# Forgetting attention: the values of two groups of heads in one GEMM, and two paddings

## The chip, the cores and the metric

The kernel runs on one core of one Trainium2 chip. The metric is the device time of one execution in microseconds. A core has TensorE (PE in the profile, its weight loads PEld), VectorE (DVE), ScalarE (ACT), GpSimd (POOL) and SyncE (SP), each with its own queue, and DMA engines.

## What is computed

One layer on 512 tokens of width 1024, all in float32: a modulated FFN, a mixing layer with two branches (an mLSTM and a forgetting attention), and a second modulated FFN. The change is in the attention. Cut to it:

```python
z = u @ w_mix + b_mix                      # q_f, k_f, v_f: 16 heads of 64 each
def forgetting_attention(q, k, v, f_pre, q_g, k_g):
    q = rms_norm(q, q_g); k = rms_norm(k, k_g)
    F = cumsum(log_sigmoid(f_pre))         # over the tokens
    logits = q @ k.T / 8 + (F[query] - F[key])      # causal
    p = softmax(logits)
    return p @ v
```

The FFN is `(silu(u @ w_a) * (u @ w_b)) @ w_out`.

## The kernel before

**Numbers.** A float32 product is made of three fp32r products: each operand is split into a high and a low part (`split`, L96 on ACT and L98 on DVE for weights), and `mm3` (L115 to L117) issues high x high, high x low and low x high into the same PSUM bank. A tile's name with h or l at its end is such a part: `wh`, `wl` are weights, `uh`, `ul` the normalized activations, eight tiles of 128 channels each.

**Buffers.** PSUM is cut in two pools of four banks each, `g` for the large GEMMs and `t` for the small ones. A tile of a pool with a tag shares that tag's buffers with the tiles before it and waits until one is free. Every pool's tiles start where the ones before them end; `pad` takes a few bytes so that later tiles start elsewhere.

**Order.** A scheduler puts each engine's instructions into one fixed order when the kernel is built, from priorities and its own estimate of durations. The program's text gives the priorities: the attention's steps call `advance(fill, n)` between them, which takes `n` steps of a generator of large GEMM pieces, so that PE has work while DVE and ACT do the softmax.

**The first FFN's products.** `pair_out` multiplies ready sums of hidden channels (tiles `ph`, `pl`, and `pt` for the last three pairs) with weights in `product` (L472 to L474). The ready sums are the stationary operand, 128 columns of them, and 512 columns of weights move. The first FFN's tiles lie in pools above the pool `tp` ("f1t"), which holds a `pad` of 96 bytes; the second FFN uses the same code with other pools.

**The attention's groups.** The 16 heads are worked in four groups of four. `fox_qkv(g)` makes a group's tokens-by-channels tiles: first q and k (one GEMM of 512 columns, four chunks of 256 rows of weights), evacuated to `tk` and normalized, then the values (a GEMM of 256 columns in two chunks of 512 rows). `u_gemm_tokens` runs a chunk over four token blocks, with one `g` bank for each block, and yields after every second block; in the last chunk `done` evacuates each bank. For the values that is a bias add on DVE (`vg`, L1110), then for each pair of heads a copy on ACT (`fvt`, L1113) and a subtraction on DVE (L1114), into the tiles `fvt`, which share the tag "vm" (six buffers) with the mLSTM's values `vm`.

**A head.** `fox_t` transposes q and k of two heads (L1144) and splits them (`fq`, `fk`, `klz`; L1146 to L1154), `fox_s` makes scores of a head in four `t` banks (L1173, L1174) and reduces them on DVE (L1176, L1180), `fox_p` scales and transposes the probabilities (L1202) and splits them into `Ph`, `Pl` (L1200, L1201), `fox_o` multiplies with the values (L1232) and adds up (`yt`, `yb`; L1235, L1236).

**The fill.** While the last two mLSTM heads are worked, the fill is `fox_qkv(0)`, in round g of four heads it is `fox_qkv(g + 1)`, and in the last round the gated mLSTM output `y_a`. `with_gates` puts a number of gate GEMMs behind each (`gate`: two steps of twelve matmuls of 512 columns, one `g` bank, a tanh `tg` on ACT, L1268).

Of the kernel before, what the change touches and what calls it, by code (L numbers as in the profile page):

```python
# [11 lines left out]
F32 = mybir.dt.float32  # L12
F32R = mybir.dt.float32r
# [7 lines left out]
P = 128  # L21
T = 512
NT = 4
D = 1024
NK = 8
# [9 lines left out]
QM, KM, VM, OM, IG, FG, QF, KF, VF, FFG, GA, GB = (  # L35
    0, 512, 1024, 2048, 3072, 3076, 3080, 4104, 5128, 6152, 6168, 7192)
# [12 lines left out]
class Layer:  # L49
# [96 lines left out]
    def consts(self, tp):  # L146
        nc, cp, A = self.nc, self.cp, self.A
        row = lambda ap: ap.rearrange("o (r p) -> (o r) p", p=P)
        bm = A["b_mix"]

        self.rowsC = tp.tile([32, P], F32, name="rowsC")
        for r, ap in ((0, row(A["c"])), (8, row(A["ffn1_norm_g"])), (16, row(A["b_ada"][:, 0:2048]))):
            nc.scalar.dma_start(self.rowsC[r:r + ap.shape[0], :], ap)
        self.ident = cp.tile([P, P], F32, name="ident")
        make_identity(nc, self.ident)
        self.one = cp.tile([P, 1], F32, name="one")
        nc.gpsimd.memset(self.one, 1.0)
        self.rowsA = tp.tile([P, P], F32, name="rowsA")
        put = lambda r, ap: nc.gpsimd.dma_start(self.rowsA[r:r + ap.shape[0], :], ap)
        put(R_N2, row(A["mix_norm_g"]))  # L160
        put(R_N3, row(A["ffn2_norm_g"]))
        put(R_CW, A["conv_w"][0].rearrange("j (m p) -> (j m) p", p=P))
        put(R_CB, row(A["conv_b"]))
        put(R_QK, row(bm[:, 0:1024]))
        put(R_GG, row(bm[:, GA:GA + 2048]))
        put(R_MG, A["mlstm_norm_g"][0].rearrange("h (r p) -> (h r) p", p=P))
        put(R_FQ, A["fox_q_norm_g"][0].rearrange("(r h) p -> r (h p)", h=2))
        put(R_FK, A["fox_k_norm_g"][0].rearrange("(r h) p -> r (h p)", h=2))
        put(R_OM, row(bm[:, OM:OM + 1024]))
        self.gbias = cp.tile([96, 1], F32, name="gbias")  # L170
        nc.gpsimd.memset(self.gbias, 0.0)
        for r, o, n in ((0, IG, 4), (32, FG, 4), (64, FFG, 16)):
            nc.gpsimd.dma_start(self.gbias[r:r + n, :], bm[0, o:o + n].unsqueeze(1))

        warm = tp.tile([P, 1], F32, name="warm")
        self.pad(tp, 96)
        nc.scalar.activation(warm, self.one, AF.Silu)
        self.oneR = cp.tile([P, 2, 33], F32R, name="oneR")
        nc.scalar.activation(self.oneR, self.one.unsqueeze(2).to_broadcast([P, 2, 33]), AF.Copy, scale=0.0)
        for h in range(2):  # L180
            nc.scalar.activation(self.oneR[:, h, 32 * h:32 * h + 1], self.one, AF.Copy)
        self.mod_d = self.dp.tile([9, D], F32, name="mod_d")
        self.pad(cp, 64)
# [809 lines left out]
    def v_mlstm(self, half, ap, ip):  # L993
        nc, w = self.nc, self.A["w_mix"][0]
        bb = self.bias_bcast([(VM + half * 512, 512)], ip)
        vt = []
        for i in range(2):
            pair = [self.vp.tile([P, NT, 264], F32R, name=self.nm("vm"), tag="vm", bufs=6)[:, :, 0:258] for _ in range(2)]
            nc.scalar.activation(pair[0][:, :, 256:258], self.onz, AF.Copy)
            nc.scalar.activation(pair[1][:, :, 256:258], self.onz, AF.Copy, scale=0.0)  # L1000
            vt.append(pair)
        def done(tb, ps):
            f = self.tmp(ip, "vf")
            nc.vector.tensor_tensor(f, ps, bb, op=ADD)
            for i in range(2):
                hi, lo = vt[i]
                s = slice(i * 256, (i + 1) * 256)
                nc.scalar.activation(hi[:, tb, 0:256], f[:, s], AF.Copy)
                nc.vector.tensor_tensor(lo[:, tb, 0:256], f[:, s], hi[:, tb, 0:256], op=SUB)
        def mk(ch):  # L1010
            def make():
                wh, wl = self.w_mov(w, ch * 256, VM + half * 512)
                return wh, wl, 2 * ch, 2
            return make
        self.vt[2 * half:2 * half + 2] = vt
        yield from self.u_gemm_tokens([mk(c) for c in range(4)], 512, done)
# [60 lines left out]
    def fox_qkv(self, g, ip):  # L1077

        nc, sp, w = self.nc, self.sp, self.A["w_mix"][0]
        o = g * 256  # L1080
        bb = self.bias_bcast([(QF + o, 256), (KF + o, 256)], ip)
        tok = [ip.tile([P, 512], F32, name=self.nm("tk"), tag="tok", bufs=4) for _ in range(NT)]
        ss = sp.tile([P, NT, 8], F32, name=self.nm("fs"), tag="fs", bufs=2)
        def done(tb, ps):
            nc.vector.tensor_tensor(tok[tb], ps, bb, op=ADD)  # L1085
            j = self.tmp(ip, "fj")
            nc.scalar.activation(j, tok[tb], AF.Square)
            nc.vector.tensor_reduce(ss[:, tb, :], j.rearrange("p (h d) -> p h d", h=8), AX.X, ADD)
        def mk(ch):
            def make():  # L1090
                sh = [P, 2, 512]
                rows = w[ch * 256:(ch + 1) * 256]
                r = self.raw(sh, [(lambda t, i=i: t[:, :, i * 256:(i + 1) * 256],
                                   rows[:, c + o:c + o + 256].rearrange("(k p) n -> p k n", p=P))
                                  for i, c in enumerate((QF, KF))])
                wh, wl = self.split(r, sh)
                return wh, wl, 2 * ch, 2
            return make
        yield from self.u_gemm_tokens([mk(c) for c in range(4)], 512, done)
        v = sp.tile([P, NT * 8], F32, name=self.nm("fv"), tag="fv", bufs=2)  # L1100
        nc.vector.tensor_scalar(v, ss.rearrange("p b h -> p (b h)"), 1.0 / 64, EPS, op0=MUL, op1=ADD)
        r = self.rsqrt(v, NT * 8)
        for tb in range(NT):
            t3 = tok[tb].rearrange("p (h d) -> p h d", h=8)
            nc.vector.tensor_tensor(t3, t3, r[:, tb * 8:(tb + 1) * 8].unsqueeze(2).to_broadcast([P, 8, 64]), op=MUL)
        bv = self.bias_bcast([(VF + o, 256)], ip)
        vt = [self.vp.tile([P, NT, 2, P], F32R, name=self.nm("fvt"), tag="vm", bufs=6) for _ in range(2)]
        def donev(tb, ps):
            f = ip.tile([P, 256], F32, name=self.nm("vg"), tag="t2", bufs=3)
            nc.vector.tensor_tensor(f, ps[:, :256], bv[:, :256], op=ADD)  # L1110
            for pr in range(2):
                f2 = f[:, pr * P:(pr + 1) * P].rearrange("p (h d) -> p h d", h=2)
                nc.scalar.activation(vt[pr][:, tb, :, 0:64], f2, AF.Copy)  # L1113
                nc.vector.tensor_tensor(vt[pr][:, tb, :, 64:P], f2, vt[pr][:, tb, :, 0:64], op=SUB)  # L1114
        def mkv(ch):
            def make():
                sh = [P, 4, 256]
                r = self.raw(sh, [(lambda t: t, w[ch * 512:(ch + 1) * 512, VF + o:VF + o + 256]
                                   .rearrange("(k p) n -> p k n", p=P))])
                wh, wl = self.split(r, sh)  # L1120
                return wh, wl, 4 * ch, 4
            return make
        self.fx[g] = (tok, vt)
        yield from self.u_gemm_tokens([mkv(c) for c in range(2)], 256, donev)

    def fox_t(self, p, ap):

# [168 lines left out]
    def run(self):  # L1296
# [61 lines left out]
        with tc.tile_pool(name="heads", bufs=1) as self.vp, tc.tile_pool(name="att", bufs=1) as ip:  # L1358
# [27 lines left out]
            def with_gates(gen, n):  # L1386
                yield from gen
                for m, i in (next(gates) for _ in range(n)):
                    yield from self.gate(m, i, ip)
            for h0, n, fill in ((0, 3, with_gates(self.v_mlstm(1, ip, ip), 2)), (2, 4, with_gates(self.fox_qkv(0, ip), 2))):  # L1390
                for f, h in ((self.mlstm_w, h0), (self.mlstm_w, h0 + 1), (self.mlstm_h, h0), (self.mlstm_h, h0 + 1)):
                    f(h, ip)
                    advance(fill, n)
                    if f == self.mlstm_h and h == 2:
                        self.fox_t(0, yp)
                advance(fill, 99)
            for n in range(18):
                if n % 4 == 0 and n < 16:
                    advance(fill, 99)
                    g = n // 4  # L1400
                    fill = with_gates(self.fox_qkv(g + 1, ip), 4 if g < 2 else 3) if g < 3 else (s for m in range(NK) for s in self.y_a(m, yp, ip))
                last = n >= 12
                if n < 16:
                    self.fox_s(n, ip)
# [98 lines left out]
```

## Time and profile before

| what | value |
|---|---|
| median of 3 runs | 1333.47 us (1333.05 to 1334.53) |
| profiled execution | 1333.42 us |
| its span | 1331.6 us |
| PE busy | 1312.8 us, 6468 matmuls |
| DVE busy | 945.8 us |
| ACT busy | 631.3 us |

The span is the time from the first to the last instruction of the profiled execution; its own time has some 1.8 us around it. In a group's row stand the line, engine, operation, tiles (result<-operands), shape and count, then busy time in us and the mean duration in ns, then idle time of the engine ahead of it and what ended that. In a timeline row stand start and duration in us, then the same names. In a row of windows stand the window, its length, then busy us (and instructions) of PE, PEld, DVE, ACT and POOL, the clock, the share of the DMA engines and GB/s. Matmuls are pipelined, so that a matmul's record is longer than its distance to the next.

### The profile page before, as it was taken

The numbers are of one execution on the slowest core, as the hardware profiler recorded it, in microseconds if no ns is written. First come the engines' busy times: TensorE is split into PE (matmuls) and PEld (weight loads), VectorE is DVE, ScalarE is ACT, GpSimd is POOL, SyncE is SP. The second block draws the span as 40 slices with busy tenths as digits, with TensorE's granted clock in tenths as the row PEclk, the third lists the DMA queues.
The fourth block names the chain that finished last, engine by engine and source line by source line (L and its number), as shares of the span: only waits on it lengthen the run. The fifth ranks groups of instructions, "written<-read, shape, count | busy, mean of one in ns | idle before, by whom it ended". The sixth has DMA issues, their size and how long they took to land.

```text
span 1331.6 us, 17899 instructions
## 1 busy us (share of the span) xinstructions
PE 1312.8 (99%) x6468; PEld 1102.8 (83%) x6468; DVE 945.8 (71%) x1775; ACT 631.3 (47%) x1080; POOL 85.9 (6%) x140
## 2 busy tenths in 40 slices
PE   7999999999999999999999999999999999999998
PEld 6688888888888888988888878888888888888887
DVE  6777677688678867887685976777676565655655
ACT  5533433336557735566575686432354333433442
POOL 2000000001020000000000000002120000000000
PEclk9999999999999999999999999999999999999999
DMA  9776576777662434443343442787537555444474
GB/s 297 226 269 220 168 236 205 255 234 239 215 161 81 135 111 124 134 116 123 80 143 88 112 124 77 227 256 236 160 101 267 185 175 163 145 151 150 153 253 147
DMA packets 228621, 231.11 MB, mean 174 GB/s; under 512 B 12274, under 2 KB 183954, under 8 KB 228532
## 3 DMA queue, kind: packets, MB, share of 16 engines
q1 hardware_dynamic: 217428, 186.34, 46.4%
q0 software_dynamic: 11040, 43.61, 8.8%
q8 instruction: 51, 0.84, 0.2%
q14 instruction: 38, 0.31, 0.1%
q10 hardware_dynamic: 64, 0.02, 0.0%
HBM read 199.97 MB, written 29.95 MB: 173 GB/s over the span
## 4 chain that ended last, share of the span: by engine, by line
PE 91%; DVE 3%; ACT 2%; DMA 2%; issue 1%; SPq 0%; POOL 0%; ACTq 0%; DVEq 0%; POOLq 0%
PE g L117 21%; PE g L116 21%; PE g L115 21%; PE t L472 2%; PE t L474 2%; PE t L473 2%; PE t L1232 2%; PE t L446 1%; PE t L447 1%; PE t L445 1%; PE t L1202 1%; PE t L115 1%; PE t L117 1%; PE t L116 1%; PE g L829 1%
## 5 line engine op out<-in xcount | busy, mean ns | idle before, releaser
L96 ACT ACTIVATE wh<-raw 128x1024 fp32r<-128x1024 f32 x218 | 226.5, 1043 | 387.6 <-PE g L116 97.4
L116 PE MATMUL g<-ul,wh 128*128 128x512 f32 (+2 forms) x984 | 369.9, 376 | 1.1 <-DVE ul L255 0.8
L115 PE MATMUL g<-uh,wh 128*128 128x512 f32 (+2 forms) x984 | 370.1, 377 | 0.1
L117 PE MATMUL g<-uh,wl 128*128 128x512 f32 (+2 forms) x984 | 369.4, 376 | 0.2 <-DVE wl L98 0.2
L98 DVE TENSOR_TENSOR wl<-raw,wh 128x1024 fp32r<-128x1024 f32 x218 | 263.4, 1211 | 141.5 <-ACT wh L96 130.1
L116 PEld LDWEIGHTS g<-ul,wh 128*128 128x128 f32 (+1 forms) x984 | 185.0, 188 | 34.7 <-DVE ul L255 1.0
L117 PEld LDWEIGHTS g<-uh,wl 128*128 128x128 f32 (+1 forms) x984 | 184.9, 188 | 34.0 <-DVE wl L98 0.4
L115 PEld LDWEIGHTS g<-uh,wh 128*128 128x128 f32 (+1 forms) x984 | 184.7, 188 | 34.2 <-ACT sl L368 0.5
L115 PE MATMUL g<-wh,uh 128*128 128x512 f32 (+1 forms) x320 | 111.9, 350 | 0.0
L116 PE MATMUL g<-wl,uh 128*128 128x512 f32 (+1 forms) x320 | 111.0, 347 | 0.0
L117 PE MATMUL g<-wh,ul 128*128 128x512 f32 (+1 forms) x320 | 111.0, 347 | 0.0
L296 DVE SCALAR_TENSOR_TENSOR acc<-raw,ccol,acc 128x1024 f32<-128x1024 f32 (+1 forms) x63 | 66.0, 1065 | 43.0 <-DMA raw<-in_w_ada_dram 42.7
L117 PEld LDWEIGHTS g<-wh,ul 128*128 128x128 f32 x320 | 60.5, 189 | 7.8
L115 PEld LDWEIGHTS g<-wh,uh 128*128 128x128 f32 x320 | 60.5, 189 | 7.7 <-DVE tk L1085 0.5
L116 PEld LDWEIGHTS g<-wl,uh 128*128 128x128 f32 x320 | 60.5, 189 | 7.3
L369 DVE TENSOR_TENSOR hp<-g,sl 128x512 f32<-128x512 f32 x43 | 29.5, 689 | 51.6 <-PE g L117 50.8
L116 PE MATMUL g<-yl,wh 128*128 128x512 f32 x128 | 49.8, 389 | 0.0
L115 PE MATMUL g<-yl,wh 128*128 128x512 f32 x128 | 49.8, 389 | 0.0
L117 PE MATMUL g<-yl,wl 128*128 128x512 f32 x128 | 49.8, 389 | 0.0
L422 ACT ACTIVATE wh<-rw 128x1024 fp32r<-128x1024 f32 x22 | 23.3, 1058 | 49.0 <-issue 31.5
L1184 ACT ACTIVATE S<-S,mn 128x128 f32<-128x128 f32 (+1 forms) x64 | 35.5, 556 | 16.0 <-DVE mn L1176 8.9
L1446 POOL TENSOR_TENSOR sg<-sg,ta 128x512 f32<-128x512 f32 x8 | 13.6, 1694 | 452.4 <-DMA raw<-in_w_branch_b_dram 421.2
(339 smaller groups left out, 2252.1 us busy)
## 6 DMA issues: line engine op xcount, KB each, us to landing
raw<-in_ffn_w_in_dram SPq DMA_DIRECT2D x82, 512.0 KB, 4.7
raw<-in_w_ada_dram SPq DMA_DIRECT2D x56, 512.0 KB, 4.3
raw<-in_w_mix_dram SPq DMA_DIRECT2D x48, 512.0 KB, 3.9
rw<-in_ffn_w_out_dram POOLq DMA_DIRECT2D x20, 1024.0 KB, 6.8
S_d<-rw POOLq DMA_DIRECT2D x22, 768.0 KB, 4.0
raw<-S_d SPq DMA_DIRECT2D x30, 512.0 KB, 3.6
raw<-in_w_mix_dram SPq DMA_DIRECT2D x32, 256.0 KB, 3.9
ar<-in_w_ada_dram SPq DMA_DIRECT2D x14, 512.0 KB, 7.6
```

Of the source, the lines that this page charges most:

```text
L96: self.last_hi = nc.scalar.activation(hi, src, AF.Copy)
L98: self.last_lo = self.last_wl = (eng or nc.vector).tensor_tensor(lo, src, hi, op=SUB)
L115: mm(ps, lh, rh, start=start, stop=False)
L116: mm(ps, lh, rl, start=False, stop=False)
L117: self.last_mm = mm(ps, ll, rh, start=False, stop=stop)
L296: nc.vector.scalar_tensor_tensor(a, r[:, cut(i)], self.ccol[:, k:k + 1], a, op0=MUL, op1=ADD)
L369: nc.vector.tensor_tensor(h, ps_b[:, c0:c1], s[:, :c1 - c0], op=MUL)
L472: mm(ps[t], a[0], wh[:, k, :], start=first and c + k == 0, stop=False, skip_group_check=True)
L473: mm(ps[t], a[0], wl[:, k, :], start=False, stop=False, skip_group_check=True)
L474: mm(ps[t], a[1], wh[:, k, :], start=False, stop=end, skip_group_check=True)
L1184: nc.scalar.activation(S[:, ws], S[:, ws], AF.Exp, scale=-1.0, bias=m, accum_out=sm[:, qb:qb + 1])
L1232: nc.tensor.matmul(po[:, q0:], vt[pr][:, kb, i % 2, :], Px[:, o:o + T - q0], start=n == 1, stop=n == 8)
```

## The change

The values of two groups (eight heads) are made in one GEMM of 512 columns, in the `fox_qkv` of the even group; the odd group's `fox_qkv` ends after q and k and takes the upper two of the pair's four `fvt` tiles. The numbers of gates behind each `fox_qkv` change, so that each round's fill keeps its number of steps. The pad in `tp` grows by 128 bytes, and a `vm` tile's token block from 264 to 272 elements, so that a tile of that tag takes 4352 bytes and not 4224.

```diff
         warm = tp.tile([P, 1], F32, name="warm")
-        self.pad(tp, 96)
+        self.pad(tp, 224)
...
-            pair = [self.vp.tile([P, NT, 264], F32R, name=self.nm("vm"), tag="vm", bufs=6)[:, :, 0:258] for _ in range(2)]
+            pair = [self.vp.tile([P, NT, 272], F32R, name=self.nm("vm"), tag="vm", bufs=6)[:, :, 0:258] for _ in range(2)]
...
-        bv = self.bias_bcast([(VF + o, 256)], ip)
-        vt = [self.vp.tile([P, NT, 2, P], F32R, name=self.nm("fvt"), tag="vm", bufs=6) for _ in range(2)]
+        if g % 2:
+            self.fx[g] = (tok, self.fx[g - 1][1][2:4])
+            return
+        bv = self.bias_bcast([(VF + o, 512)], ip)
+        vt = [self.vp.tile([P, NT, 2, P], F32R, name=self.nm("fvt"), tag="vm", bufs=6) for _ in range(4)]
         def donev(tb, ps):
-            f = ip.tile([P, 256], F32, name=self.nm("vg"), tag="t2", bufs=3)
-            nc.vector.tensor_tensor(f, ps[:, :256], bv[:, :256], op=ADD)
-            for pr in range(2):
+            f = self.tmp(ip, "vg")
+            nc.vector.tensor_tensor(f, ps, bv, op=ADD)
+            for pr in range(4):
...
         def mkv(ch):
             def make():
-                sh = [P, 4, 256]
-                r = self.raw(sh, [(lambda t: t, w[ch * 512:(ch + 1) * 512, VF + o:VF + o + 256]
-                                   .rearrange("(k p) n -> p k n", p=P))])
-                wh, wl = self.split(r, sh)
-                return wh, wl, 4 * ch, 4
+                wh, wl = self.w_mov(w, ch * 256, VF + o)
+                return wh, wl, 2 * ch, 2
             return make
         self.fx[g] = (tok, vt)
-        yield from self.u_gemm_tokens([mkv(c) for c in range(2)], 256, donev)
+        yield from self.u_gemm_tokens([mkv(c) for c in range(4)], 512, donev)
...
-(2, 4, with_gates(self.fox_qkv(0, ip), 2))
+(2, 4, with_gates(self.fox_qkv(0, ip), 0))
...
-fill = with_gates(self.fox_qkv(g + 1, ip), 4 if g < 2 else 3)
+fill = with_gates(self.fox_qkv(g + 1, ip), (6, 2, 5)[g])
```

PE, second round of heads (group 1), where the scores of head 6 (`t_6348` and its neighbours) follow pieces of group 2's values (`g_6283`, `g_6284`), in the order before. In it 64 matmuls of the values stand between the first four transposes of head 4 (L1202) and these scores.

```order
L117 MATMUL g_6283<-wh_6373,ul_2970 128x256
L115 MATMUL g_6284<-wh_6373,uh_2959 128x256
L116 MATMUL g_6284<-wl_6374,uh_2959 128x256
L117 MATMUL g_6284<-wh_6373,ul_2967 128x256
L115 MATMUL g_6284<-wh_6373,uh_2960 128x256
L1173 MATMUL t_6348<-fk_6206,fq_6204 128x256
L1173 MATMUL t_6353<-fk_6206,fq_6204 128x256
L1173 MATMUL t_6359<-fk_6206,fq_6204 128x384
```

The same place in the order of the changed kernel (lines are one higher there from L1114 on, and more inside `fox_qkv`).

```order
L116 MATMUL g_6176<-wl_6242,uh_2957 128x512
L117 MATMUL g_6176<-wh_6241,ul_2965 128x512
L115 MATMUL g_6176<-wh_6241,uh_2958 128x512
L1174 MATMUL t_6216<-fk_6096,fq_6094 128x256
L1174 MATMUL t_6221<-fk_6096,fq_6094 128x256
L1174 MATMUL t_6227<-fk_6096,fq_6094 128x384
```

Ahead of these scores now stand 34 matmuls of 512 columns behind the first four transposes. At the same place of the third round 64 matmuls of group 3's values become 34 of the gates.

DVE, end of group 2's values in the order before: the evacuation of the last two token blocks (`vg`, then `fvt` high and low), with a weight split between (`wl`), and the sum of a head's output behind it (`yb`).

```order
L1110 TENSOR_TENSOR vg_6425<-g_6285,bb_6279 128x256
L1110 TENSOR_TENSOR vg_6443<-g_6286,bb_6279 128x256
L98 TENSOR_TENSOR wl_6591<-raw_6588,wh_6590 128x1024
L1114 TENSOR_TENSOR fvt_6281<-vg_6425,fvt_6281 128x2x64
L1114 TENSOR_TENSOR fvt_6282<-vg_6425,fvt_6282 128x2x64
L1114 TENSOR_TENSOR fvt_6281<-vg_6443,fvt_6281 128x2x64
L1114 TENSOR_TENSOR fvt_6282<-vg_6443,fvt_6282 128x2x64
L1236 TENSOR_TENSOR yb_3462<-t_6449,yt_6458 64x512
```

The same in the order of the changed kernel, where this evacuation stands one head later.

```order
L1113 TENSOR_TENSOR vg_6413<-g_6177,bb_6169 128x512
L1113 TENSOR_TENSOR vg_6429<-g_6178,bb_6169 128x512
L98 TENSOR_TENSOR wl_6664<-raw_6660,wh_6663 128x1024
L1117 TENSOR_TENSOR fvt_6171<-vg_6413,fvt_6171 128x2x64
L1117 TENSOR_TENSOR fvt_6172<-vg_6413,fvt_6172 128x2x64
L1117 TENSOR_TENSOR fvt_6173<-vg_6413,fvt_6173 128x2x64
L1117 TENSOR_TENSOR fvt_6174<-vg_6413,fvt_6174 128x2x64
L1117 TENSOR_TENSOR fvt_6171<-vg_6429,fvt_6171 128x2x64
L1117 TENSOR_TENSOR fvt_6172<-vg_6429,fvt_6172 128x2x64
L1117 TENSOR_TENSOR fvt_6173<-vg_6429,fvt_6173 128x2x64
L1117 TENSOR_TENSOR fvt_6174<-vg_6429,fvt_6174 128x2x64
L1237 TENSOR_TENSOR yb_3462<-t_6458,yt_6467 64x512
```

Eight subtractions now stand between the last add and `yb`, where four stood.

More of the change, by code (lines that the diff above doesn't have):

```diff
@@ L1389, in with_gates @@
                     yield from self.gate(m, i, ip)
-            for h0, n, fill in ((0, 3, with_gates(self.v_mlstm(1, ip, ip), 2)), (2, 4, with_gates(self.fox_qkv(0, ip), 2))):
+            for h0, n, fill in ((0, 3, with_gates(self.v_mlstm(1, ip, ip), 2)), (2, 4, with_gates(self.fox_qkv(0, ip), 0))):
                 for f, h in ((self.mlstm_w, h0), (self.mlstm_w, h0 + 1), (self.mlstm_h, h0), (self.mlstm_h, h0 + 1)):
@@ L1400, in run @@
                     g = n // 4
-                    fill = with_gates(self.fox_qkv(g + 1, ip), 4 if g < 2 else 3) if g < 3 else (s for m in range(NK) for s in self.y_a(m, yp, ip))
+                    fill = with_gates(self.fox_qkv(g + 1, ip), (6, 2, 5)[g]) if g < 3 else (s for m in range(NK) for s in self.y_a(m, yp, ip))
                 last = n >= 12
```

## The prediction

> **What bounds the kernel.** I read the page's busy shares and its chain first, because they say whether anything but TensorE has to be looked at; then the groups by shape, for counts and durations; then the timeline of PE, for what the pages cannot give: the distance from one matmul's start to the next.
>
> ```profile
> span 1331.6 us, 17899 instructions
> PE 1312.8 (99%) x6468; PEld 1102.8 (83%) x6468; DVE 945.8 (71%) x1775; ACT 631.3 (47%) x1080; POOL 85.9 (6%) x140
> PEclk9999999999999999999999999999999999999999
> PE 91%; DVE 3%; ACT 2%; DMA 2%; issue 1%; SPq 0%; POOL 0%; ACTq 0%; DVEq 0%; POOLq 0%
> ```
>
> PE is busy for 99% of the span, at the full clock in all 40 slices, and 91% of the chain that ended last is PE's own work. So an edit counts by what it does to the stream of matmuls; work moved on DVE and ACT counts only where PE comes to wait for it. A matmul's recorded duration is no price here, since the records overlap. Starts are the price:
>
> ```profile
> L115 PE MATMUL g<-wh,uh 128*128 128x256 f32 x128 | 36.7, 287 | 0.0
> 506.13 0.39 PE L115 MATMUL g<-wh,uh 128*128 128x512 f32 x1
> 515.65 0.39 PE L115 MATMUL t<-qkh,qkh 128*128 128x512 f32 x1
> 532.08 0.28 PE L115 MATMUL g<-wh,uh 128*128 128x256 f32 x1
> 543.60 0.27 PE L1144 MATMUL t<-ident,tk 128*128 128x128 f32 x1
> ```
>
> From 506.13 to 515.65 stand 42 matmuls of 512 columns (seven pieces of six): 9.52 / 42 = 0.2267 us each. From 532.08 to 543.60 stand the 96 matmuls of the first group's values: 11.52 / 96 = 0.1200 us each. Two narrow ones cost 0.2400, one wide one 0.2267, although both compute the same 512 columns.
>
> **The values' GEMM.** The quoted 256-column group is one line of three (L115, L116, L117), 128 each: 384 matmuls, 96 for each of four groups. The change makes 192 of 512 columns. Before 384 x 0.1200 = 46.1 us; after 192 x 0.2267 = 43.5: 2.6 us less. But a wide run that follows narrow work starts slower:
>
> ```profile
> 504.74 0.40 PE L115 MATMUL g<-wh,uh 128*128 128x512 f32 x1
> ```
>
> The six from 504.74 to 506.13 took 1.39 us, 0.2317 each, 0.005 over the later ones. The new values' matmuls come in 16 pieces of twelve, many right behind score or transpose matmuls. If every piece has six slow ones, 16 x 6 x 0.005 = 0.5 us comes back; if none has, nothing. Taking the middle: **-2.3 us** (ends -2.1 and -2.6).
>
> The Trainium skill's page "TensorE: Matmul & The Clock Gate", section "Back-to-back issue gap", gives a warm matmul N / 2.4 + 2.5 ns. By it two of 256 would cost 218.3 ns and one of 512 215.8, and the step would bring 192 x 2.5 ns = 0.5 us. The rows above show 240.0 and 226.7, so here the measurement decides and the 2.6 us stands.
>
> **The pads.** In the built program the first FFN's tiles of ready sums (ph, pl, pt) begin 128 bytes past a multiple of 256, the second FFN's on a multiple; in the changed program both are on one. The code that reads them is the same, so the second FFN is the control:
>
> ```profile
> 334.34 0.40 PE L472 MATMUL g<-wh,ph 128*128 128x512 f32 x1
> 349.68 0.39 PE L472 MATMUL t<-wh,ph 128*128 128x512 f32 x1
> 1281.86 0.39 PE L472 MATMUL g<-wh,ph 128*128 128x512 f32 x1
> 1296.82 0.39 PE L472 MATMUL t<-wh,ph 128*128 128x512 f32 x1
> ```
>
> Each pair of rows frames the same product, 11 sums x 2 row blocks x 3 = 66 matmuls: 15.34 us in the first FFN (0.2324 each), 14.96 in the second (0.2267). Three such products make 198 matmuls: 3 x 0.38 = **-1.1 us** if the start address is the whole difference, 0 if it is something else in that stage. I take the address, since 0.2267 is also what the aligned matmuls cost in the row at 506.13. Half of the values' tiles (fvt, four of eight) lie 128 past as well; of the weights' loads from them 16 precede matmuls of 512 columns: 16 x 0.0057 = **-0.1 us**. For the values' tiles of the mLSTM (vm), read as 258-column moving operands, no row shows a price; the nearest are the 256-column rows at 532.08, at 0.1200 whatever stands before them, so I take 0 (their 120 matmuls at 0.0057 would be 0.7 either way).
>
> The Trainium skill's page "SBUF — State Buffer" names only cachelines of 16 bytes, and calls its section "Operand start alignment" a matter "about legality, not speed". By it 128 bytes are as good as 256 and the pads bring nothing; that is a rival below. The control rows speak against it, though they show two stages and not one stage twice.
>
> **The evacuation, the loads, the moved gates.** The bias add goes from 16 of 256 columns to 8 of 512, the splits stay 32 on each engine:
>
> ```profile
> L1110 DVE TENSOR_TENSOR vg<-g,bb 128x256 f32<-128x256 f32 x16 | 6.4, 419 | 0.0
> L1085 DVE TENSOR_TENSOR tk<-g,bb 128x512 f32<-128x512 f32 x16 | 10.5, 685 | 9.7 <-PE t L1144 9.6
> L1114 DVE TENSOR_TENSOR fvt<-vg,fvt 128x128 fp32r<-128x128 f32 x32 | 7.7, 286 | 0.0
> L1113 ACT ACTIVATE fvt<-vg 128x128 fp32r<-128x128 f32 x32 | 7.6, 297 | 3.2 <-DVE vg L1110 3.2
> ```
>
> DVE's total falls from 16 x 0.419 = 6.7 to 8 x 0.685 = 5.5 us, off the path. What changes is where it falls: a token block then costs 0.685 + 4 x 0.286 = 1.83 us on DVE instead of 0.419 + 2 x 0.286 = 0.99, four blocks in a row, 3.4 us more at groups 0 and 2, and 4.0 us less at groups 1 and 3. Is there room?
>
> ```profile
> 560.00:565.00 5.00, 5.00 (x23) 4.13 (x23) 3.01 (x13) 3.07 (x10) 0.00 (x0) 1.00 0.77 233
> 565.00:570.00 5.00, 5.00 (x23) 4.13 (x22) 2.65 (x7) 1.06 (x1) 0.00 (x0) 1.00 0.64 200
> 670.00:675.00 5.00, 5.00 (x35) 4.62 (x34) 5.00 (x20) 4.01 (x12) 0.00 (x0) 1.00 0.22 52
> 675.00:680.00 5.00, 5.00 (x29) 4.26 (x28) 5.00 (x14) 2.91 (x9) 0.00 (x0) 1.00 0.34 69
> ```
>
> The third figure of a row is DVE's. After group 0 it is half idle for ten us, so that burst is covered. In group 2 it is full for ten us, and there the count goes thus. After the last values' matmul PE has a gate's half (12 x 0.2267), eight output matmuls (about 1.3), another half and eight transposes (about 0.9): 7.6 us before a transpose needs the bank that yb (L1237) frees. DVE must do in that time, by the new order, two adds (1.4), a weight split (1.2), eight subtractions (2.3) and yb (0.7): 5.6 us. Covered with 2.0 us to spare; if the cover fails, yb is late, and the transposes L1203 wait. Weights: two loads of 512 KB for each group become four for each pair, so the bytes, the splits (one for each two steps) and SP's issues stay; rows of 2 KB replace rows of 1 KB. Four bias broadcasts become two, read only by the adds at the end. DMA is at 0.22 to 0.77 of its engines in these windows; I cost all of it at 0. The gates only change places (2, 2, 4, 4, 3 become 2, 0, 6, 2, 5), each still 48 x 0.2267 us on PE, and the steps of each round stay 16, 20, 20, 18.
>
> **The waits at the turns.** In the second and third round PE waits for ACT's fk:
>
> ```profile
> 666.04 0.28 PE L115 MATMUL g<-wh,uh 128*128 128x256 f32 x1
> 666.65 0.68 PE L1173 MATMUL t<-fk,fq 128*128 128x256 f32 x3 [0.33 <-ACT fk L1154]
> 739.35 0.28 PE L115 MATMUL g<-wh,uh 128*128 128x256 f32 x1
> 739.96 0.50 PE L1173 MATMUL t<-fk,fq 128*128 128x256 f32 x2 [0.34 <-ACT fk L1154]
> 661.71 0.60 ACT L1200 ACTIVATE Ph<-t 128x512 fp32r<-128x512 f32 x1 [1.08 <-PE t L1202]
> 665.31 0.63 ACT L1150 ACTIVATE fk<-ft 64x512 fp32r<-64x512 f32 x1
> ```
>
> 0.61 - 0.12 = 0.49 us each time. Ahead of these scores stand 64 narrow matmuls (7.68 us); in the new order 34 wide ones (34 x 0.2267 = 7.71), of the values in round two, of gates in round three. PE arrives as early as before, so the waits stay. ACT's chain to fk starts with Ph, for which ACT idled until the transposes L1202; these stand behind 27 narrow matmuls (3.24) and now behind 15 wide ones (3.40). So fk comes 0.16 later, twice: **+0.3 us** (between 0 and +0.6).
>
> **The sum** is -2.3 - 1.1 - 0.1 + 0.3 = -3.2 us. What follows on PE simply comes earlier. The profiled execution took 1333.42 us (span 1331.6 and 1.8 around it), 0.05 under the median of 1333.47, so **1330.2 us**, 0.25% faster. By measurement, a difference under 0.2% (2.7 us) can hardly be told from none.
>
> **Rivals.** *The pads do nothing:* -2.3 + 0.3 = -2.0, 1331.4 us. For it: the first FFN's stage has other neighbours than the second's. Against it: 0.38 us in a product of nothing but matmuls. *The burst is partly uncovered:* DVE is full where group 2's values end, and if its queue runs 1 to 2 us behind there, the sum is about -1.7: 1331.7. *The waits for fk go:* with no values' copies on ACT in rounds one and three, fk may come earlier; 2 x 0.49 and the 0.3 go, 1328.9. *Slower:* one mechanism, the doubled evacuation in DVE's queue ahead of the score reductions and yb. If the whole extra 3.4 us lands on PE at both groups, 6.7 us against 3.2 gained: 1336.9. It starts to count when DVE is more than 2.0 us behind at group 2, and decides at 3.2 us in sum; half-idle DVE after group 0 speaks against it.
>
> **Chances.** The forecast as summed 0.50; pads nothing 0.12; burst partly uncovered 0.19; waits gone 0.12; slower 0.07. Even the slow end of the first (-2.1, -1.1, +0.6) is 2.6 us, at the edge of 0.2%. Faster by over 0.2%: 0.50 and 0.12, 0.62; within: 0.12 and 0.19, 0.31; slower 0.07. The range reaches from a little under the case of the waits gone with the full 2.6 (1328.5) to the burst's 1332.0; it leaves out the slower case and the edges.
>
> **What the changed profile would show.** The values as x64 on each of three lines at 128x512, and about 43.5 to 44 us from their starts; the first FFN's product framed as above at 14.96 us; waits for fk near 0.5 us in rounds two and three; no PE wait on yb, Pl or g behind the values' evacuation. I am wrong on the pads if that product stays at 15.3, and on the cover if PE waits for DVE near the end of group 2's values.

## The result, and the profile after

The changed kernel takes 1329.54 us (median of five, 1328.19 to 1330.11) against 1334.31 (1333.05 to 1334.90) for the kernel before on the same chip: ratio 0.9968, interval 0.9957 to 0.9978. The forecast was 1330.2 (1328.5 to 1332.0). The profiled execution is the fastest of the five, 1328.19 us. In two later comparisons, side by side, the ratio was 0.9976 and 0.9971 (below). So the change makes the kernel 0.24 to 0.32% faster, 3.5 to 4.8 us; the forecast was 0.25%.

The page of the changed kernel: busy time, and the group that holds the values (the span is 1326.4 us).

```profile
PE 1308.5 (99%) x6276; PEld 1091.2 (82%) x6276; DVE 943.2 (71%) x1767; ACT 630.4 (48%) x1080; POOL 85.6 (6%) x140
...
L115 PE MATMUL g<-wh,uh 128*128 128x512 f32 x256 | 100.6, 393 | 0.0
```

There are 192 matmuls fewer, PE is still the bound, and the 256-column group is gone: the 256 here are the 192 that this form had and 64 of the values. The timeline of PE, after (start, duration, then what ran):

```profile
333.27 0.39 PE L472 MATMUL g<-wh,ph 128*128 128x512 f32 x1
...
348.23 0.39 PE L472 MATMUL t<-wh,ph 128*128 128x512 f32 x1
...
434.51 0.27 PE L945 MATMUL t<-ident,ggm 64*128 64x64 f32 x1
...
529.85 0.39 PE L115 MATMUL g<-wh,uh 128*128 128x512 f32 x1
...
540.75 0.38 PE L1145 MATMUL t<-ident,tk 128*128 128x128 f32 x2
...
662.54 0.39 PE L115 MATMUL g<-wh,uh 128*128 128x512 f32 x1
663.17 0.39 PE L1174 MATMUL t<-fk,fq 128*128 128x256 f32 x1 [0.24 <-ACT fk L1155]
...
1276.98 0.39 PE L472 MATMUL g<-wh,ph 128*128 128x512 f32 x1
...
1321.63 0.39 PE L474 MATMUL t<-wh,pt 128*128 128x512 f32 x1
```

The first FFN's product between the two L472 rows takes 14.96 us (15.34 before). The first half of the first pair's values, 48 matmuls of 512 columns from 529.85 to 540.75, takes 10.90 us, 0.2271 each. The wait for fk in the second round is 0.63 - 0.23 = 0.40 us, and so is the third round's, from 735.20 to 735.83 (0.49 before).

To see where the time came from, the execution is cut at three marks on PE: the first framed product of the first FFN, the small transpose of the gates at L945 (between the first FFN and the attention), and the first framed product of the second FFN. Two rows of the kernel before complete its marks (334.34 and 1281.86 stand in the prediction).

```profile
436.79 0.40 PE L945 MATMUL t<-ident,ggm 64*128 64x64 f32 x3
...
1326.51 0.39 PE L474 MATMUL t<-wh,pt 128*128 128x512 f32 x1
```

| stretch, us | before | after | difference |
|---|---|---|---|
| start to the first FFN's product | 334.34 | 333.27 | -1.07 |
| that product to L945 | 102.45 | 101.24 | -1.21 |
| L945 to the second FFN's product | 845.07 | 842.47 | -2.60 |
| that product to the last matmul | 44.65 | 44.65 | 0.00 |

The third stretch holds the values, the second the first FFN's ready sums. The first stretch is not touched by the change; the experiments show whether its 1.07 us come back.

### The profile page after: what moved, and what is told of

The parts are those of the page before. It is cut to its first block, busy times and chain, and to the rows that moved or that the text cites. A ratio compares the mean times of both kernels' runs of the same rounds, so it can differ in the third digit from the quotient of the medians.

```text
span 1326.4 us, 17502 instructions
## 1 busy us (share of the span) xinstructions
PE 1308.5 (99%) x6276; PEld 1091.2 (82%) x6276; DVE 943.2 (71%) x1767; ACT 630.4 (48%) x1080; POOL 85.6 (6%) x140
## 4 chain that ended last, share of the span: by engine, by line
PE 94%; ACT 2%; DVE 2%; issue 1%; DMA 1%; SPq 0%; POOL 0%; ACTq 0%; POOLq 0%; DVEq 0%
PE g L116 22%; PE g L117 22%; PE g L115 22%; PE t L472 2%; PE t L473 2%; PE t L474 2%; PE t L1233 2%; PE t L446 2%; PE t L447 2%; PE t L445 2%; PE g L829 1%; PE t L1203 1%; PE t L116 1%; PE t L115 1%; PE t L117 1%; PE t L1174 1%
## 5 line engine op out<-in xcount | busy, mean ns | idle before, releaser
L115 PE MATMUL g<-wh,uh 128*128 128x512 f32 x256 | 100.6, 393 | 0.0
L116 PE MATMUL g<-wl,uh 128*128 128x512 f32 x256 | 99.9, 390 | 0.0
L117 PE MATMUL g<-wh,ul 128*128 128x512 f32 x256 | 99.8, 390 | 0.0
L117 PEld LDWEIGHTS g<-wh,ul 128*128 128x128 f32 x256 | 48.0, 188 | 10.2
L115 PEld LDWEIGHTS g<-wh,uh 128*128 128x128 f32 x256 | 48.1, 188 | 9.9 <-DVE tk L1085 0.4
L116 PEld LDWEIGHTS g<-wl,uh 128*128 128x128 f32 x256 | 48.1, 188 | 9.3
L1185 ACT ACTIVATE S<-S,mn 128x128 f32<-128x128 f32 (+1 forms) x64 | 35.5, 555 | 13.3 <-DVE mn L1177 7.1
```

Source lines behind the costliest of these rows:

```text
L115: mm(ps, lh, rh, start=start, stop=False)
L116: mm(ps, lh, rl, start=False, stop=False)
L117: self.last_mm = mm(ps, ll, rh, start=False, stop=stop)
L1185: nc.scalar.activation(S[:, ws], S[:, ws], AF.Exp, scale=-1.0, bias=m, accum_out=sm[:, qb:qb + 1])
```

## Experiments

Theory: the address of the stationary operand sets the pace of the FFN's products (1.1 us), the wide values bring 2.3 to 2.6 us, and the two add. First rival: the pads do nothing. Of changed lines, the edits below show only the part that differs. The first four kernels ran on one chip with the kernel before (1333.84 us, 33 runs).

**The values alone.**

```diff
-        self.pad(tp, 224)
+        self.pad(tp, 96)
...
-[P, NT, 272]
+[P, NT, 264]
```

> The changed kernel with both paddings as before (pad of 96 bytes, vm blocks of 264 elements): only the values' GEMM and the gates' places are new. My theory (the start address of the stationary tile sets the pace of the product): the values bring -2.3 to -2.6 us against the kernel before, about 0.9980 to 0.9983 of its time; the first FFN's product stays at 15.3 us for its 66 matmuls. Rival (the stage, not the address): the same gain here, but the whole gain of the change then comes from here, about 0.9968.

Measured: 1330.79 us (11 runs), ratio 0.9978 (0.9969 to 0.9987). Its marks:

```profile
334.29 0.40 PE L472 MATMUL g<-wh,ph 128*128 128x512 f32 x1
...
349.63 0.39 PE L472 MATMUL t<-wh,ph 128*128 128x512 f32 x1
...
437.05 0.27 PE L945 MATMUL t<-ident,ggm 64*128 64x64 f32 x1
...
1279.56 0.39 PE L472 MATMUL g<-wh,ph 128*128 128x512 f32 x1
```

The product is back at 15.34 us, the third stretch is 842.51: the 2.6 us belong to the values. The first stretch, 334.29, is as long as before. The medians differ by 3.05 us, 0.45 more than this stretch lost; where that lies stays open.

**The pads alone.** The kernel before with the other half of the change.

```diff
-        self.pad(tp, 96)
+        self.pad(tp, 224)
...
-[P, NT, 264]
+[P, NT, 272]
```

> The kernel before with only the two paddings changed. My theory: the first FFN's product goes from 15.34 to 14.96 us, three of them -1.1 us, with the values' tiles -1.2 to -1.4 in all, ratio about 0.9990; the values' GEMM stays at 11.5 us for each group. Rival (the pads do nothing, the first FFN's slower pace is its neighbours'): product 15.3 us, ratio 1.0000.

Measured: 1333.42 us (11 runs), ratio 0.9997 (0.9988 to 1.0005).

```profile
334.71 0.39 PE L472 MATMUL g<-wh,ph 128*128 128x512 f32 x1
...
349.68 0.39 PE L472 MATMUL t<-wh,ph 128*128 128x512 f32 x1
...
436.71 0.27 PE L945 MATMUL t<-ident,ggm 64*128 64x64 f32 x1
...
1281.69 0.39 PE L472 MATMUL g<-wh,ph 128*128 128x512 f32 x1
```

The product takes 14.97 us, as the theory says; but the second stretch is 102.00, only 0.45 under the kernel before, and so is the time (0.42). Of three times 0.38 more than half did not arrive. The third stretch, 844.98, is 0.09 shorter: what the alignment of fvt and vm brings together.

**The second FFN put off its alignment.** The changed kernel with 128 bytes at the start of the second FFN's pool.

```diff
+            self.pad(fp, 128)
```

> The changed kernel with 128 bytes put into the second FFN's pool, so that its ready sums now begin 128 past a multiple of 256 and the first FFN's do not. My theory: the second FFN's product goes from 14.96 to 15.3 us, its three products cost +1.1 us, about 1.0008 of the changed kernel's time on the same chip. Rival (the stage): its product stays at 14.96 us and the time is the changed kernel's.

Measured: 1331.51 us (11 runs), 1.17 over the changed kernel beside it, ratio to the kernel before 0.9983 (0.9974 to 0.9992).

```profile
1279.30 0.40 PE L472 MATMUL g<-wh,ph 128*128 128x512 f32 x1
...
1294.64 0.39 PE L472 MATMUL t<-wh,ph 128*128 128x512 f32 x1
...
1325.08 0.39 PE L474 MATMUL t<-wh,pt 128*128 128x512 f32 x1
```

The same product in the same stage goes from 14.96 to 15.34, and the last stretch from 44.65 to 45.78. That settles the address: it isn't the stage. Nor is it the moving operand, since the weights lie in the pool `w`, which is opened ahead of the padded pools and which no pad shifts. At the end of the kernel, where nothing waits, the whole 1.1 us shows in the time.

**The changed kernel again.**

> The changed kernel once more, for comparison on the same chip. Both effects: -2.6 for the values and -1.2 for the pads, about 3.8 us under the kernel before, ratio 0.9971. If the 1.05 us that arose ahead of 334 us belongs to the change and not to single executions, the ratio is again 0.9964 or lower.

Measured: 1330.34 us (1329.17 to 1332.42, 11 runs), ratio 0.9976 (0.9967 to 0.9985). On this chip the two halves add up: 3.05 and 0.42 us for each alone, 3.50 for both. The 1.07 us of the first stretch are not part of the change: the stretch is 333.77 here, and in all fourteen profiles of this case it lies between 333.27 and 334.85 whatever the kernel; the first profile of the changed kernel is the lowest of all. But the second stretch is 102.92 here, longer than before the change:

```profile
333.77 0.39 PE L472 MATMUL g<-wh,ph 128*128 128x512 f32 x1
...
360.19 0.44 PE L271 MATMUL t<-ident,xn 128*128 128x128 f32 x2 [1.40 <-DVE xn L241]
...
436.69 0.27 PE L945 MATMUL t<-ident,ggm 64*128 64x64 f32 x1
```

PE stands for 1.40 us at L271, the transposes of the next layer's normalized input, waiting for DVE's `xn`. This wait is not in the kernel before, and it is where the pads' gain goes. It costs more than its row says. With the pads alone the row has 0.35 us, but PE takes 0.74 us from the last product's matmul to the first transpose where the first profile after takes 0.23, and the sixteen transposes take 0.10 more: 0.6 of the 0.75 us by which the second stretch is longer there (102.00 against 101.24). A later profile of the same kernel (the third, below) has it at 1.46 us and names the cause. First come ACT and DVE in that profile, then DVE in the first profile after, which has no such wait:

```profile
348.46 1.06 ACT L96 ACTIVATE wh<-raw 128x1024 fp32r<-128x1024 f32 x1 [2.03 <-DMA raw<-S_d]
...
349.56 1.23 DVE L98 TENSOR_TENSOR wl<-raw,wh 128x1024 fp32r<-128x1024 f32 x1 [1.87 <-ACT wh L96]
350.70 0.69 DVE L533 TENSOR_TENSOR rs<-g,sn 128x512 f32<-128x512 f32 x1
...
360.45 0.88 DVE L241 TENSOR_SCALAR xn<-x,rq 128x512 f32<-128x512 f32 x2
```

```profile
346.17 1.23 DVE L98 TENSOR_TENSOR wl<-raw,wh 128x1024 fp32r<-128x1024 f32 x1 [1.15 <-ACT wh L96]
347.75 0.69 DVE L533 TENSOR_TENSOR rs<-g,sn 128x512 f32<-128x512 f32 x1 [0.35 <-PE g L474]
...
357.50 0.89 DVE L241 TENSOR_SCALAR xn<-x,rq 128x512 f32<-128x512 f32 x2
```

From the residual sum `rs` to `xn` DVE needs 9.75 us in both. In the second fence `rs` waits for PE's product; in the first it stands in DVE's queue behind a weight split, which waits for ACT's high part, which waits for a load. There the load sets `xn`, and a product that ends 0.4 us earlier only makes PE wait longer. Why the load is late in one execution and not in another stays open. In the seven profiles with aligned sums and this order PE waited for `xn` 0, 0, 0.4, 0.4, 0.5, 1.4 and 1.5 us, in the four with the sums off alignment 0, 0, 0 and 0.2.

**The transposes later.** In the third product of the first FFN the hook that turns `xn` comes one chunk later.

```diff
-self.w_split(sums, 0), False, 3, hooks)
+self.w_split(sums, 0), False, 3 if final else 2, hooks)
...
-{0: scale, 2: turn}
+{0: scale, 3: turn}
```

> The changed kernel with one edit more: in the first FFN's third product the transposes of the next layer's normalized input (L271, from xn) stand six matmuls of 512 columns later on PE, 1.36 us. In the runs so far PE waited there for DVE's xn 1.4 us (changed kernel again), 0.4 (pads only), 0.2 (values only), 0.5 (second FFN's sums moved), not at all in the two first profiles. Theory (part of what the pads give in the first FFN is given back at this wait, since the residual sums stand in DVE's queue behind weight splits that wait for their loads): the wait is 0.2 us or less, and the time is 0.4 to 1.2 us under the changed kernel's, ratio to the kernel before 0.9965 to 0.9970. Rival (the wait is only moved, because what reads the transposes then comes late): the same wait appears behind, at the mixing layer's first matmuls, ratio 0.9976.

> The same, with the pad in the first FFN's pool as before (96 bytes), so that its ready sums begin 128 past a multiple of 256. Theory: with no wait at the turn to give it back at, the three products' 3 x 0.38 = 1.1 us come through whole, so this is 1.1 us slower than the kernel without this (ratio about 0.9975 where that has 0.9967). Rival (the pads are worth 0.4 us, as the difference of the runs without this edit): 0.3 to 0.5 us slower.

Measured on one chip (before: 1333.10 us, 16 runs): with the pad 1328.54 (1328.15 to 1329.12, 6 runs), ratio 0.9966 (0.9954 to 0.9978); with the old pad 1330.34 (11 runs), ratio 0.9978 (0.9969 to 0.9987). The marks with the pad, then with the old one:

```profile
333.85 0.39 PE L472 MATMUL g<-wh,ph 128*128 128x512 f32 x1
...
435.05 0.27 PE L945 MATMUL t<-ident,ggm 64*128 64x64 f32 x1
```

```profile
334.47 0.40 PE L472 MATMUL g<-wh,ph 128*128 128x512 f32 x1
...
436.72 0.27 PE L945 MATMUL t<-ident,ggm 64*128 64x64 f32 x1
```

The second stretch is 101.20 against 102.25: 1.05 us, the pads' whole price, and no wait for `xn` in either. The medians differ by 1.80; in the two profiles 0.62 of that stands ahead of the first mark, where executions vary anyway. One thing is open: in all three profiles with this edit (the third belongs to the last comparison below) the loads were early (`rs` waited for PE's product and not behind a late split), so they don't show the edit carrying a late `xn`.

**Other addresses.** Single runs, 1329.98 and 1330.18 us, with the ready sums 64 and 32 bytes past a multiple of 256 (the pad in `tp` is 288 and 256).

> The changed kernel with the first FFN's ready sums 64 bytes past a multiple of 256 instead of on one. Theory (what costs is that a weight load of 512 bytes for each partition reaches into one 256-byte line more): 15.34 us for the product of 66 matmuls, as at 128. Rivals: only multiples of 128 that aren't multiples of 256 cost, 14.96 us; or the cost goes with the distance, 15.15 us.

> The same at 32 bytes past a multiple of 256. Theory of the line: 15.34 us. If the cost goes with the distance, 15.06; if what matters is a multiple of 64, this one alone is slow.

```profile
333.95 0.40 PE L472 MATMUL g<-wh,ph 128*128 128x512 f32 x1
...
349.35 0.40 PE L472 MATMUL t<-wh,ph 128*128 128x512 f32 x1
```

```profile
334.11 0.39 PE L472 MATMUL g<-wh,ph 128*128 128x512 f32 x1
...
349.50 0.40 PE L472 MATMUL t<-wh,ph 128*128 128x512 f32 x1
```

15.40 us at 64 and 15.39 at 32: each start off a multiple of 256 that was tried costs 0.38 to 0.44 us in 66 matmuls, 6 to 7 ns each. It neither grows with the distance nor asks for multiples of 128 or 64 only. That a load then reaches into one more piece of 256 bytes fits this; the runs do not show it.

**More work in the evacuation.** For the rival that ends slower: each subtraction of the values' low parts issued twice, and four times.

```diff
-                nc.vector.tensor_tensor(vt[pr][:, tb, :, 64:P], f2, vt[pr][:, tb, :, 0:64], op=SUB)
+                for _ in range(2):      # 4 in the second kernel
+                    nc.vector.tensor_tensor(vt[pr][:, tb, :, 64:P], f2, vt[pr][:, tb, :, 0:64], op=SUB)
```

> The changed kernel with each subtraction that makes a values' tile low (L1117) issued twice (same result): 1.14 us more of DVE for each token block, 4.6 us for each pair of groups. By the prediction's count DVE had 2.0 us to spare behind group 2's values, where the last two blocks now bring 2.3 us more: PE loses 0.3 us there, nothing at group 0, so about 0.3 us over the changed kernel. Rival (the doubled evacuation is on the path already): the whole of the last two blocks, 2.3 us at both groups, 4.6 us over.

> The same with each of these subtractions four times: 3.4 us more of DVE for each token block, 6.9 us for the last two. By the count 6.9 - 2.0 = 4.9 us of new PE waits behind group 2's values, and 2 to 4 us behind group 0, where DVE was half idle for ten us: 5 to 9 us over the changed kernel. Rival (DVE has much more room than 2.0 us, since what waits for it can wait): under 2 us over.

Single runs of 1330.86 and 1330.83 us, beside 1328.65 to 1331.14 for the changed kernel on the same chip. DVE is busy for 949.4 us with two and for 962.0 with four. With four, the marks on PE; then PE's waits from 530 to 800 us (total, times, longest), first with four, where lines behind L1117 are one higher, then in the changed kernel:

```profile
435.66 0.27 PE L945 MATMUL t<-ident,ggm 64*128 64x64 f32 x1
...
1279.38 0.39 PE L472 MATMUL g<-wh,ph 128*128 128x512 f32 x1
```

```profile
PE t L1175 <- ACT fk L1156: 1.1, 4, 0.4
PE g L115 <- DVE vg L1113: 0.8, 2, 0.6
...
```

```profile
PE t L1203 <- ACT ft L1147: 0.5, 1, 0.5
PE t L1174 <- ACT fk L1155: 0.5, 2, 0.2
PE t L1174 <- DVE Pl L1202: 0.4, 1, 0.4
PE t L1174 <- DVE mn L1181: 0.2, 1, 0.2
```

962.0 - 943.2 = 19 us more of DVE work lengthen the third stretch from 842.47 to 843.72, by 1.3 us; with two, 6 us more leave it at 842.59, 0.1 longer (I had expected 0.3, the rival 4.6). What is new with four is a wait of gate matmuls for a bank that a bias add frees late (the vg row), not one for `yb`; the two rows left out are waits for `ft` and `mn`, as in the changed kernel. My 5 to 9 us were far off; the rival's "under 2" held. The timeline of DVE behind group 2's values shows one reason, first in the changed kernel, then with four:

```profile
685.68 1.71 DVE L1117 TENSOR_TENSOR fvt<-vg,fvt 128x128 fp32r<-128x128 f32 x8
...
687.58 0.69 DVE L1237 TENSOR_TENSOR yb<-t,yt 64x512 f32<-64x512 f32 x1 [0.20 <-ACT yt L1236]
```

```profile
695.12 0.70 DVE L1238 TENSOR_TENSOR yb<-t,yt 64x512 f32<-64x512 f32 x1
...
696.46 3.32 DVE L1118 TENSOR_TENSOR fvt<-vg,fvt 128x128 fp32r<-128x128 f32 x16
```

The scheduler made a new order for the longer work: `yb`, which stood behind the last two blocks' subtractions, now stands ahead of the last block's. In the kernel after, `yb` waited for ACT's `yt` and not for the subtractions ahead of it. So the runs show that this evacuation has room, not that the old order had it.

**The changed kernel and the later transposes, side by side.**

> The changed kernel on the same chip as the next. In single runs it was 3.5 us under the kernel before on one chip and 4.8 on another; with 0 to 1.5 us of waiting for xn in it I expect 3.5 to 4.2 under, ratio 0.9969 to 0.9974.

> The changed kernel with the transposes of xn six matmuls later, on the same chip as the changed kernel. Theory: no wait for xn, and 0.4 to 1.2 us under the changed kernel, ratio 0.9962 to 0.9968. Rival (its lead was the chip's): the same time as the changed kernel.

Measured (before: 1333.27 us, 10 runs): the changed kernel 1329.80 (1328.65 to 1331.14, 6 runs), ratio 0.9971 (0.9959 to 0.9983); with the later transposes 1328.30 (1328.22 to 1329.12, 5 runs), ratio 0.9965 (0.9952 to 0.9977). The intervals overlap. But over all comparisons the eleven runs with later transposes lie within 1328.15 and 1329.12, while 18 of the changed kernel's 22 lie above that, up to 1332.42. It is the best version seen, by about 1.5 us in the medians.

## Why the prediction was right, and where it was not

- **The values, -2.3: right, but the slow starts cost more than assumed, on both sides.** The third stretch lost 2.6 us in every kernel that has the wide values (842.4 to 842.5 wherever nothing else in it was changed). Not all of that is the values': about 0.2 are the two waits for fk and 0.1 the aligned fvt tiles (both below). Counted from start to start over all their runs of neighbouring matmuls, with the last of each run at the steady pace, the values take 46.5 us before and 44.1 after (44.1 without the pads, too): 2.3 less. The wide ones gave 0.6 back, more than the upper bound of 0.5. The price of 0.005 us for each slow matmul was read behind other work; behind the transposes of the probabilities it is larger:

```profile
654.20 0.50 PE L115 MATMUL g<-wh,uh 128*128 128x512 f32 x1
...
655.69 0.39 PE L115 MATMUL g<-wh,uh 128*128 128x512 f32 x1
```

  These six took 1.49 us, the first six from 529.85 on, behind the mLSTM's products, 1.37, and six at the steady pace take 1.36. The narrow values paid 0.4 us for slow starts of their own, which the prediction left out. That the sum still came out at 2.3 is luck.
  By the formula for an isolated matmul in the Trainium skill's page "TensorE: Matmul & The Clock Gate", section "Back-to-back issue gap", the step would have brought 0.5 us; the runs show 2.3. From 0.1200 and 0.2267 us one gets 0.4168 ns for each column and 13.3 ns that do not depend on the columns, and 192 x 13.3 ns is 2.55 us ahead of the slow starts. A third width agrees: for 384 columns this gives 0.173 us, and the mLSTM's matmuls of 384 columns (`t<-qkh,qkh`) start 0.173 us apart.
- **The pads, -1.1: price right, path wrong.** The framed product lost 0.37 or 0.38 us in all but one of the profiles with aligned sums (0.31 in the third of the changed kernel), and the second FFN, put off its alignment, paid the same. The step that failed is the one that let all that follows on PE simply come earlier: in the next product of ready sums stand the transposes of `xn`, and in five of seven profiles PE waited there. The pads alone brought 0.4 us. The first profile after was one of the two without this wait, so that its second stretch showed the whole price by chance. The rival drawn from the Trainium skill's page "SBUF — State Buffer", section "Operand start alignment", that the pads bring nothing (the section itself gives no times), is contradicted by the products at each of the three offsets.
- **fvt -0.1, vm 0: right.** The third stretch of the kernel with the pads alone is 0.09 us shorter. Counted from start to start without the waits, its 32 output matmuls of 512 columns that read fvt take 7.60 us against 7.67 before, and the 120 that read vm 14.62 against 14.61.
- **Later fk, +0.3: wrong.** The waits fell from 0.49 to 0.40 us. ACT's rows at the second round's turn, after and then before (Ph of before, 661.71, stands in the prediction):

```profile
658.37 0.60 ACT L1201 ACTIVATE Ph<-t 128x512 fp32r<-128x512 f32 x1 [1.29 <-PE t L1203]
...
662.49 0.63 ACT L1155 ACTIVATE fk<-ft 64x512 fp32r<-64x512 f32 x1
```

```profile
665.97 0.63 ACT L1154 ACTIVATE fk<-ft 64x512 fp32r<-64x512 f32 x1
```

  Before, the first values' matmul behind the transposes, from which the prediction counted, stands here (after, it is the row at 654.20):

```profile
657.74 0.39 PE L115 MATMUL g<-wh,uh 128*128 128x256 f32 x1
```

  Counted from these matmuls, the second fk started after 8.29 us instead of 8.23: 0.06 later, not 0.16. Ph was late as forecast (4.17 instead of 3.97), but from Ph to that fk ACT took 4.12 us instead of 4.26; why stays open. PE would have come to the scores 0.23 us after the last wide matmul (662.77) or 0.12 after the last narrow one (666.16), which is 8.57 us after those matmuls instead of 8.42: 0.15 later, where the prediction had 0.03, since the wide runs start slower. So the wait shrank by 0.09. Twice -0.09 for +0.16 is half a microsecond.
- **The evacuation, 0: right.** After the change no wait on yb or on g stands behind the values (the changed kernel's waits are shown under the experiment with more work); the largest wait for Pl between 530 and 800 us is 0.4 us (0.5 before). Whether the 2.0 us of room were counted too small, or the new orders of the two heavier kernels make the room, is not told apart.
- **The rival that the waits at the turns go: out.** They shrank by 0.09 us each and did not go.
- **The sum.** The third stretch's 2.6 us (the fk waits and fvt are in it) and 0.4 (the pads alone) to 1.2 (no wait for `xn`) make 3.0 to 3.8; the forecast was 3.2. It had the gain 0.5 us too low at the fk waits and up to 0.7 too high at the pads. These cancel, so that the close number is luck in part. The medians lost 4.8, 3.5 and 3.5. In the first pair of profiles 1.07 us more lie ahead of the first mark, which the other profiles of the changed kernel do not repeat.

## What to carry over

In this kernel two matmuls of 256 columns cost 13 ns more than one of 512. So joining a GEMM's moving side to 512 columns brings this overhead once for each matmul that goes, less what more slow starts behind transposes cost, as long as the evacuation's larger burst finds room. Count such starts in the form before as well as in the form after. Stationary tiles are worth starting on multiples of 256 bytes, by the offsets tried here. A gain in a stretch is only worth what the next meeting point lets through: look, behind the stretch that becomes shorter, for the first PE instruction that waits for another engine, and ask whether that engine's queue is paced by PE or by loads. And take several profiles, since one of each kernel had 1.07 us of difference where nothing had been changed.

## What the runs showed of the hardware

- A stationary operand of 128 fp32r columns (512 bytes for each partition) that starts 32, 64 or 128 bytes off a multiple of 256 costs 6 to 7 ns for each matmul of 512 columns, whatever its distance (15.34 to 15.40 us against 14.96 for 66).
- The start of an execution, up to the first FFN's product, varies by 1.6 us between executions (333.27 to 334.85), at the full clock.
- Late loads come and go from execution to execution of one program: the split on DVE ahead of `rs` started 12.9 us behind the first mark in one profile of the changed kernel and 15.1 in another (346.17 and 349.56 us), where ACT's high part ahead of it waited 2.03 us for its load.
- A run of 512-column matmuls starts slower behind narrower work, and how much depends on what stands ahead: six took 1.37 us behind the mLSTM's products and 1.49 behind transposes, 1.36 at the steady pace.
